# The moving operand of a PE-bound kernel read in 16-byte pieces, by turns from its two halves

## The chip, the cores and the metric

The kernel runs on one core of a Trainium2 chip. Its time is the device time of one execution in microseconds (us); several executions are timed and their median counts. One further execution was recorded by the hardware profiler; the profile and the trace are of that one.

A core has a matrix engine (TensorE, called PE in the profile, with its weight loads as PEld), a vector engine (VectorE, DVE), a scalar engine (ScalarE, ACT), a general engine (GpSimd, POOL) and a queue that issues DMAs (SyncE, SP). They run side by side and wait for each other by semaphores. Operands lie in SBUF, 128 partitions with a row of bytes each; PE writes its results to PSUM, in banks of 512 float32 numbers (2 KB) per partition.

## What is computed

A trunk of two pre-norm residual layers over 512 tokens of 1024 features, in float32, each followed by a squared-ReLU MLP, with RMSNorm at the end. Cut to what matters:

```python
for i in range(2):
    h = rmsnorm(x, norm_mix_g[i])
    h = chunked_spatial_gating(h, ...) if i == 0 else retention(h, ...)
    x = x + h
    h = rmsnorm(x, norm_ffn_g[i])
    a = jax.nn.relu(h @ mlp_w1[i])          # 1024 -> 4096
    x = x + (a * a) @ mlp_w2[i]             # 4096 -> 1024
return rmsnorm(x, final_norm_g)
```

The gating layer has matmuls of 1024 to 4096 and 2048 to 1024 features; the retention has projections of 1024 to 6144 and 2048 to 1024, and inside each of its four heads products of tokens with tokens (scores) and of scores with values.

## The kernel before, in words

Every large product is a sum of three matmuls. Each operand is split into a high part, rounded to PE's float32r format, and a low part, which is the rest; high times high, high times low and low times high are added up in the same PSUM bank. The helper `mm3` (line 213) issues these three: L215, L216 and L217. Its arguments are the PSUM tile `ps`, the stationary operand's two parts `ah` and `al` (128 columns), and the moving operand's two parts `bh` and `bl` (up to 512 columns). A matmul contracts over the 128 partitions, so a product over 1024 features is eight calls of `mm3` into one bank.

Two arrangements use it. With features as the output's partitions (`mm_f`, L303, by `feat`, and `mm_o`, L307, by `out_piece`), a 128x128 piece of weights is stationary and the 512 tokens of the activations move: names `hH`, `hL` (normed input), `aH`, `aL` (MLP activations), `yH`, `yL` (mixer outputs). With tokens as the partitions (`tokens`, L339), 128 tokens are stationary and 512 columns of the weights move: `wH` and `wL`. In the retention's `scores` (L729) and `av` (L749) the moving operand has 512, 384, 256 or 128 columns, since the causal mask leaves less for later chunks. The outputs are named `v`, `u`, `o` (gating layer), `up`, `dn`, `dt` (MLP), `qk`, `vv`, `g`, `sc`, `av`, `ro` (retention). 1912 calls of `mm3` have a moving operand of 512 columns: 5736 matmuls. A few others do not go through it, among them the first 96 matmuls of the gating layer (L562), the norm's sums and spreads (L271, L272, L290, L291), the gate's products `sg` (L474, 128 columns each) and the transposes.

Weights stream in through two 1 MB buffers `raw` (L157), loaded from the SP queue. ACT rounds a piece to `wH` (L179), DVE subtracts to get `wL` (L183); `refill` does so some pieces ahead of PE. PSUM has six banks for accumulation and two for the rest, and results are taken out by DVE and ACT while PE works on other banks. The order is written out by hand: each `step` issues its matmuls, then the preparation of later weights and the pending evacuations.

A tile `fill` of 320 numbers (L130) is never used. It stands ahead of `xT`, `hH` and `hL` in memory and pushes them to multiples of 2 KB. In the built program the moving operand of each 512-column matmul starts at a multiple of 2048 bytes within its partition, so that the two halves of its 2 KB are the two kilobytes of an aligned pair.

Of the kernel before, what the change touches and what calls it, by code (L numbers as in the profile page):

```python
# [78 lines left out]
def trunk(ctx, tc, x, norm_mix_g, norm_ffn_g, a_w_in, a_b_in, a_v_norm_g, a_w_s, a_b_s, a_w_out,  # L79
# [132 lines left out]

    def mm3(ps, ah, al, bh, bl, start, stop):

        nc.tensor.matmul(ps, lhsT=ah, rhs=bh, start=start, stop=False)  # L215
        nc.tensor.matmul(ps, lhsT=ah, rhs=bl, start=False, stop=False)  # L216
        nc.tensor.matmul(ps, lhsT=al, rhs=bh, start=False, stop=stop)  # L217
# [85 lines left out]
    def mm_f(p, ps, bH, bL, ks, last):  # L303
        for k in ks:
            mm3(ps, p.hi[:, k, :], p.lo[:, k, :], bH[k], bL[k], k == 0, k == last)

    def mm_o(p, t, ps, bH, bL):  # L307
        ts = slice(t * P, (t + 1) * P)
        for k in range(4):
            mm3(ps, p.hi[:, k, ts], p.lo[:, k, ts], bH[:, k, :], bL[:, k, :], k == 0, k == 3)  # L310
# [28 lines left out]
    def tokens(plist, bufs, evac, name, behind=None, last=None):  # L339

        accs = {}
        behind = behind or {}

        def one(i):
            def run(p):
                if i == 0:
                    for n in range(NT):
                        accs[n] = acc(f"{name}_{n}")
                aH, aL = bufs()
                for n in range(NT):  # L350
                    s = slice(n * P, (n + 1) * P)
                    for k in range(2):
                        kk = 2 * i + k
                        mm3(accs[n], aH[kk][:, s], aL[kk][:, s], p.hi[:, k, :], p.lo[:, k, :], kk == 0, kk == 7)
                advance()
                refill()
                if i in behind:
                    behind[i]()
                if i == 3:
                    for n in range(NT):  # L360
                        launch(evac(n, accs[n]))
            return run

        for i, p in enumerate(plist[:2] if last else plist):
            step(one(i), p)
        if last:
            step(lambda *ps: last(bufs, accs, evac, *ps), *plist[2:])
# [593 lines left out]
    for k in range(2):  # L961
        p = order[0]
# [56 lines left out]
```

## Time and profile before

| | |
|---|---|
| median of 3 runs | 1406.9 us (1406.83 to 1407.25) |
| the profiled execution's own time | 1407.72 us |
| its span, first to last instruction | 1406.0 us |
| mean granted clock of PE | 0.998 |
| HBM traffic over the span | 95 GB/s |

The profile's page gives the busy time of each engine, the span in 40 slices with a digit for the busy tenths, the chain of work that ended last, and the costliest groups of instructions. In a group's row stand the source line, engine, operation, output and inputs, shapes and count, then the total busy time in us, the mean duration of one in ns, and the idle time of the engine just ahead of them. A matmul's duration is the time that it is in flight; the next starts before it ends. What a matmul costs in a stream is therefore read from the timeline, as the distance from its start to the next one's. A row of the table by stretches has the stretch and its length, then busy time and count of PE, PEld, DVE, ACT and POOL, the granted clock, the DMA engines' share and GB/s.

### The profile page before, as it was taken

Reading aid. Unit: us, or ns where it says so; the run is one execution under the profiler, and the core shown is the slowest. Engines: PE = TensorE matmul, PEld = TensorE weight load, DVE = VectorE, ACT = ScalarE, POOL = GpSimd, SP = SyncE. Lnnn points to the kernel's source line nnn. Section 1 sums busy time; section 2 is a strip of 40 time slices with the busy share of each in tenths; the row PEclk is TensorE's granted clock in tenths of the full one; section 3 lists DMA queues with packets and bytes.
Section 4 is the critical chain, followed back from the end, with each engine's and each line's share of the span. In section 5 each row is a group of like instructions: output and inputs, shape, how many; then the busy total and the mean of one; then the engine's idle time right before and its main releaser. Section 6 shows DMA issues by size and latency. Waiting matters only on the chain.

```text
span 1406.0 us, 15372 instructions
## 1 busy us (share of the span) xinstructions
PE 1390.5 (99%) x6290; PEld 1155.4 (82%) x6290; DVE 793.0 (56%) x1102; ACT 507.2 (36%) x721; POOL 127.7 (9%) x98
## 2 busy tenths in 40 slices
PE   8999999999999999999999999999999999999997
PEld 7888888888888888888888888888888888888885
DVE  6757765775444445476647574564685443434335
ACT  4656633334413223123334323333334422313222
POOL 3010111220000000011111100110130000000002
PEclk9999999999999999999999999999999999999999
DMA  6332222232223322423222131132122332232221
GB/s 225 109 116 90 72 90 88 81 120 90 90 90 104 106 90 90 148 89 108 90 78 72 60 120 60 62 118 90 61 90 91 120 104 90 93 117 91 90 90 60
DMA packets 106101, 135.23 MB, mean 96 GB/s; under 512 B 2400, under 2 KB 79792, under 8 KB 105776
## 3 DMA queue, kind: packets, MB, share of 16 engines
q1 hardware_dynamic: 106000, 134.26, 29.4%
q8 instruction: 49, 0.80, 0.2%
q14 instruction: 20, 0.16, 0.0%
q10 hardware_dynamic: 32, 0.01, 0.0%
HBM read 132.16 MB, written 2.10 MB: 95 GB/s over the span
## 4 chain that ended last, share of the span: by engine, by line
PE 96%; DVE 3%; POOL 0%; ACT 0%; DMA 0%; issue 0%; SPq 0%; ACTq 0%; DVEq 0%
PE up L217 8%; PE up L216 8%; PE up L215 8%; PE dn L217 4%; PE dn L216 4%; PE dn L215 4%; PE dt L216 4%; PE dt L217 4%; PE dt L215 4%; PE g L215 2%; PE qk L215 2%; PE vv L216 2%; PE g L216 2%; PE vv L215 2%; PE g L217 2%; PE vv L217 2%
## 5 line engine op out<-in xcount | busy, mean ns | idle before, releaser
L183 DVE TENSOR_TENSOR wL<-raw,wH 128x1024 fp32r<-128x1024 f32 x239 | 305.9, 1282 | 112.8 <-PE dt L216 65.5
L179 ACT CAST wH<-raw 128x1024 fp32r<-128x1024 f32 x239 | 249.7, 1045 | 264.7 <-PE dt L217 114.9
L215 PE MATMUL up<-hH,wH 128*128 128x512 f32 x480 | 187.2, 390 | 0.0
L217 PE MATMUL up<-hH,wL 128*128 128x512 f32 x480 | 186.8, 389 | 0.0
L216 PE MATMUL up<-hL,wH 128*128 128x512 f32 x480 | 186.8, 389 | 0.0
L631 DVE TENSOR_TENSOR aH<-r 128x512 fp32r<-128x512 f32 x64 | 45.0, 703 | 159.5 <-ACT r L629 159.4
L216 PEld LDWEIGHTS up<-hL,wH 128*128 128x128 f32 x480 | 90.1, 188 | 18.7
L215 PEld LDWEIGHTS up<-hH,wH 128*128 128x128 f32 x480 | 90.1, 188 | 18.7
L217 PEld LDWEIGHTS up<-hH,wL 128*128 128x128 f32 x480 | 90.1, 188 | 18.7
L215 PE MATMUL dn<-aH,wH 128*128 128x512 f32 x256 | 99.6, 389 | 0.0
L216 PE MATMUL dn<-aL,wH 128*128 128x512 f32 x256 | 99.6, 389 | 0.0
L217 PE MATMUL dn<-aH,wL 128*128 128x512 f32 x256 | 99.6, 389 | 0.0
L215 PE MATMUL dt<-wH,aH 128*128 128x512 f32 x256 | 99.6, 389 | 0.0
L216 PE MATMUL dt<-wL,aH 128*128 128x512 f32 x256 | 99.6, 389 | 0.0
L217 PE MATMUL dt<-wH,aL 128*128 128x512 f32 x256 | 99.6, 389 | 0.0
L629 ACT ACTIVATE r<-up 128x512 f32<-128x512 f32 x60 | 35.9, 598 | 166.7 <-PE up L217 166.7
L239 POOL TENSOR_TENSOR ssq<-ssq,sq 128x512 f32<-128x512 f32 x28 | 43.0, 1537 | 401.6 <-ACT sq L238 401.3
L501 DVE TENSOR_TENSOR xs<-dn,wide 128x512 f32<-128x512 f32 x32 | 22.1, 692 | 74.5 <-PE dn L217 74.5
L215 PEld LDWEIGHTS dt<-wH,aH 128*128 128x128 f32 x256 | 48.0, 188 | 10.1
L216 PEld LDWEIGHTS dn<-aL,wH 128*128 128x128 f32 x256 | 48.0, 188 | 10.0
L215 PEld LDWEIGHTS dn<-aH,wH 128*128 128x128 f32 x256 | 48.0, 188 | 10.0
L216 PEld LDWEIGHTS dt<-wL,aH 128*128 128x128 f32 x256 | 48.0, 188 | 9.9
(271 smaller groups left out, 2709.5 us busy)
## 6 DMA issues: line engine op xcount, KB each, us to landing
raw<-in_mlp_w_dram SPq DMA_DIRECT2D x64, 1024.0 KB, 5.1
raw<-in_b_w_in_dram SPq DMA_DIRECT2D x24, 1024.0 KB, 5.0
raw<-in_a_w_in_dram SPq DMA_DIRECT2D x14, 1024.0 KB, 5.2
raw<-in_a_w_out_dram SPq DMA_DIRECT2D x8, 1024.0 KB, 4.9
raw<-in_b_w_out_dram SPq DMA_DIRECT2D x8, 1024.0 KB, 4.9
raw<-in_a_w_in_dram SPq DMA_DIRECT2D x8, 256.0 KB, 6.7
out_dram<-out SPq DMA_DIRECT2D x8, 256.0 KB, 2.1
xr<-in_x_dram SPq DMA_DIRECT2D x3, 512.0 KB, 6.6
```

Of the source, the lines that this page charges most:

```text
L179: nc.scalar.copy(out=p.hi, in_=p.raw.tile[p.view])
L183: nc.vector.tensor_sub(out=p.lo, in0=p.raw.tile[p.view], in1=f32(p.hi))
L215: nc.tensor.matmul(ps, lhsT=ah, rhs=bh, start=start, stop=False)
L216: nc.tensor.matmul(ps, lhsT=ah, rhs=bl, start=False, stop=False)
L217: nc.tensor.matmul(ps, lhsT=al, rhs=bh, start=False, stop=stop)
L239: nc.gpsimd.tensor_tensor(out=state["ssq"], in0=state["ssq"], in1=sq, op=ALU.add)
L501: nc.vector.tensor_mul(t, ps, r2bc)
L629: nc.scalar.activation(r, ps, AF.Relu)
L631: nc.vector.tensor_mul(h, r, r)
```

## The change

Where the moving operand has 512 columns, `mm3` views the output and both moving operands through another access pattern:

```diff
     def mm3(ps, ah, al, bh, bl, start, stop):
 
+
+        if bh.shape[1] == 512:
+            ps, bh, bl = (v.rearrange("p (h l f) -> p l h f", h=2, f=4) for v in (ps, bh, bl))
         nc.tensor.matmul(ps, lhsT=ah, rhs=bh, start=start, stop=False)
         nc.tensor.matmul(ps, lhsT=ah, rhs=bl, start=False, stop=False)
         nc.tensor.matmul(ps, lhsT=al, rhs=bh, start=False, stop=stop)
```

The 512 columns are taken as 2 halves of 64 groups of 4. PE now reads columns 0 to 3, then 256 to 259, then 4 to 7, then 260 to 263, and so on: 16 bytes from each half by turns. The output is written through the same pattern, so that each column's result lies where it lay before. The bytes, the tiles, their places and the engines' other instructions are the same. The matmuls of 384, 256 and 128 columns and those outside of `mm3` keep their pattern.

No instruction changes its place. These are rows of PE's order of work in the MLP of layer 0, of before; `up_0` is the accumulator, `hH` and `hL` the moving parts, `wH` and `wL` the stationary weights:

```order
L215 MATMUL up_0_2632<-hH_101,wH_2546 128x512
L216 MATMUL up_0_2632<-hL_109,wH_2546 128x512
L217 MATMUL up_0_2632<-hH_101,wL_2547 128x512
L215 MATMUL up_0_2632<-hH_102,wH_2546 128x512
L216 MATMUL up_0_2632<-hL_110,wH_2546 128x512
```

And the same place of the changed kernel, whose line numbers are three higher:

```order
L218 MATMUL up_0_2632<-hH_101,wH_2546 128x64x2x4
L219 MATMUL up_0_2632<-hL_109,wH_2546 128x64x2x4
L220 MATMUL up_0_2632<-hH_101,wL_2547 128x64x2x4
L218 MATMUL up_0_2632<-hH_102,wH_2546 128x64x2x4
L219 MATMUL up_0_2632<-hL_110,wH_2546 128x64x2x4
```

The rows, their operands and their order are the same; only the shape of the access pattern differs.

## The prediction

> **What bounds the kernel now.** I read the page's busy table and its rows of slices first, then the chain that ended last, then the matrix engine's waits, and then the timeline of the matrix engine (PE) at single instructions.
>
> ```profile
> span 1406.0 us, 15372 instructions
> PE 1390.5 (99%) x6290; PEld 1155.4 (82%) x6290; DVE 793.0 (56%) x1102; ACT 507.2 (36%) x721; POOL 127.7 (9%) x98
> PE   8999999999999999999999999999999999999997
> PEclk9999999999999999999999999999999999999999
> PE 96%; DVE 3%; POOL 0%; ACT 0%; DMA 0%; issue 0%; SPq 0%; ACTq 0%; DVEq 0%
> ```
>
> PE is busy in every slice, its clock is granted in full, and it makes up 96% of the chain that set the end. A busy share alone would not prove that the matmuls stream without holes, because matmuls overlap, so the waits and the timeline have to say it. The waits of PE by who released them, with total, times and longest:
>
> ```profile
> PE xt L397 <- DMA xr<-in_x_dram: 1.8, 1, 1.8
> PE warm L958 <- POOL ident masks.py:199: 1.4, 1, 1.4
> PE bc_h L290 <- DVE dg_h L286: 0.9, 3, 0.3
> PE st_mix L272 <- POOL st_mix L263: 0.9, 1, 0.9
> ```
>
> That is 5.0 us in 1406. Now the timeline of PE in layer 0's MLP (start, duration):
>
> ```profile
> 329.98 0.39 PE L217 MATMUL up<-hH,wL 128*128 128x512 f32 x1
> ...
> 344.94 0.39 PE L217 MATMUL up<-hH,wL 128*128 128x512 f32 x1
> ```
>
> Between these two rows lie 66 intervals, all of 0.22 or 0.23 us: 14.96 / 66 = 0.2267 us from one 512-column matmul to the next. The 0.39 us printed as a duration is how long one is in flight, not what it costs. So what bounds the kernel is the rate at which 512 columns go through PE, and the change touches exactly that.
>
> **How much of the time the touched matmuls are.** mm3 is called 1912 times with 512 columns, three matmuls each: 5736 of the 6290. At 0.2267 us they take 5736 x 0.2267 = 1300 us of the span. Every nanosecond added to or taken from each is 5.74 us of the kernel. That lever is why even a tiny effect here would be seen: about 0.2% of the time, 2.8 us, is the least that a measurement of this kernel tells from no change, and that is 0.49 ns per matmul.
>
> **What one column costs, and what is left over.** The same lines run matmuls of other widths in the retention's scores, so the profile has durations of the same form at several sizes:
>
> ```profile
> L217 PE MATMUL sc<-qkH,qkL 128*128 128x512 f32 x8 | 3.1, 389 | 0.0
> L217 PE MATMUL sc<-qkH,qkL 128*128 128x384 f32 x8 | 2.7, 340 | 0.0
> L217 PE MATMUL sc<-qkH,qkL 128*128 128x256 f32 x8 | 2.3, 283 | 0.0
> ```
>
> From 256 to 512 columns the time in flight grows by 106 ns, 0.414 ns a column. 512 columns at that rate are 212.0 ns; the measured interval is 226.7. So 14.7 ns of each matmul are not explained by its columns at this slope (an estimate: the two halves of the slope, 57 and 49 ns for 128 columns, differ by 8 ns). Is that a fixed price of an instruction, or one that grows with what is streamed? Narrow matmuls tell:
>
> ```profile
> 717.36 0.33 PE L215 MATMUL av<-pH,vvH 128*128 128x384 f32 x1
> 717.53 0.34 PE L216 MATMUL av<-pL,vvH 128*128 128x384 f32 x1
> ...
> 718.25 0.22 PE L215 MATMUL av<-pH,vvH 128*128 128x128 f32 x1
> 718.31 0.28 PE L216 MATMUL av<-pL,vvH 128*128 128x128 f32 x1
> ```
>
> The first 128-column matmul is followed after 0.06 us; its columns at 0.414 are 53 ns, so some 7 ns are left (to the timeline's 10 ns). The 384-column one is followed after 0.17 us, 159 ns of columns and some 11 left. The remainder gets smaller with fewer columns, so at least part of it comes while columns are streamed. Taken as lost column times, 14.7 / 0.414 = 35 per matmul, one in about 15 columns, some 60 bytes of a partition's row. I can't see in this trace whether that is the read of the moving operand, the write of the result, or neither.
>
> **The change, part by part.** (1) It removes and adds no instruction and no DMA, and moves none: on every engine the built program has the same rows in the same order, and the touched matmuls differ in the shape of two access patterns alone (128x512 becomes 128x64x2x4). (2) The order in which PE takes the columns changes: 4 columns (16 bytes) from the first kilobyte, 4 from the second, and so on: 128 pieces per matmul where there was one run of 2048 bytes. (3) The PSUM side is written in the same order, so each result lands where it did before, and accumulation and evacuation are untouched. (4) The stationary operand is untouched; its load is beside the matmul:
>
> ```profile
> L216 PEld LDWEIGHTS up<-hL,wH 128*128 128x128 f32 x480 | 90.1, 188 | 18.7
> ```
>
> 188 ns in flight in an interval of 227; a matmul made as short as its columns, 212 ns, would still cover it. (5) A longer pattern to decode costs nothing that shows: the 0.06 us step above says that PE can start a new instruction well within a 227 ns interval.
>
> So the price is 5736 times whatever a jump of 1 KB every 16 bytes does to the stream. No matmul in the trace has such a pattern; all read and write one run. Bounds from the nearest rows: below, the whole remainder goes, 5736 x 14.7 = -84 us. Above, a column takes as long as where PE is fed by weight loads, the slowest steady rate of 128-column operands here (this is a piece of the chain):
>
> ```profile
> 220.27 0.89 PE sg L474 x8
> ```
>
> 0.89 / 8 = 0.111 us for 128 columns, 0.87 ns a column, 445 ns for 512: +218 ns each, +1252 us. I take a price of zero. The reason: what PE reads and writes per piece is still whole and consecutive, four columns in a run, the same bytes in the same number of 16-byte pieces, and the nearest row, the 512-column matmul itself, already streams them at within 14.7 ns of its column rate. With zero, the profiled execution stays at its span of 1406.0 us and its own time of 1407.72; the median of the runs shown is 1406.9, 0.8 us below that execution, and the forecast is made for it: 1406.9 us.
>
> [...]
>
> **The rivals.**
>
> *The remainder goes (faster).* If the 14.7 ns come from reading neighbouring pieces one behind the other, taking turns between two places a kilobyte apart may hide it. For it: the remainder grows with the columns. Against: if it is a limit on the data read per time, the order does not matter. Price: -14.7 x 5736 = -84 us, 1323 us. Nothing else takes over as bound: DVE is the next busiest, and in its fullest stretch it has room.
>
> ```profile
> 1000.00:1100.00 100.00, 99.66 (x454) 82.06 (x453) 74.75 (x112) 40.88 (x60) 13.24 (x9) 1.00 0.28 90
> ```
>
> DVE's 74.75 us (the third busy time of the row) would have to fit into 93.5, and the DMA engines stand at a 0.28 share. [...]
>
> *A jump costs a column's time on the read side (slower).* Today's remainder is one lost column in about 15. If it is lost each time the read leaves a stretch of some 64 bytes, then 16-byte pieces lose one every 4 columns: 128 x 0.414 = 53.0 ns in place of 14.7, +38.3 ns, +220 us: 1627 us. It decides from the point where a jump costs over 14.7 / 128 = 0.11 ns. For it: the size of the remainder fits. Against: a read of 16 bytes gives PE work for four columns, 1.66 ns, in which the next address can be fetched.
>
> *The result's write can't follow (slower still).* Each touched matmul adds its result to a PSUM bank in the new order. If each new piece costs a column on top of today's interval, it is +53.0 x 5736 = +304 us, 1711 us; at the rate of the weight-fed rows above, 2659 us. For it: no matmul in the trace writes in pieces, so nothing shows that the write side has room. [...]
>
> That the change does nothing at all is excluded: the patterns stand in the built program.
>
> **How the numbers follow.** No effect: 0.44, at 1406.9, its own range 1404.1 to 1409.7 (0.2% either way). The remainder goes, in whole or in part: 0.22, from 1323 up; one run is the simplest order that a reader of memory can be built for, so that a gain over it seems less likely than a loss. A jump on the read side, in whole or in part: 0.20, up to 1627. The write side, or a read that is worse than one column a jump: 0.14, above that. Leaving out the faster case would alone leave out more than 2 in 10; so the range runs from 1323 to 1627 and leaves out the 0.14 at the top. Faster 0.22, same 0.44, slower 0.20 + 0.14 = 0.34.
>
> **What would show it.** Right: intervals of 0.2267 us in the up stage at the same place of the timeline, the widths of the scores unchanged, and the same span. [...] One look at two neighbouring starts decides. The forecast is wrong if that interval moves by over half a nanosecond.

## The result, and the profile after

The changed kernel takes 1537.74 us (median of 4 runs, 1537.49 to 1538.03) against 1407.08 us of the kernel before in the same comparison: a ratio of 1.0926, with a 95% interval of 1.0907 to 1.0945. It is slower by 130.7 us, where the forecast was no change. The time lies inside of the stated range; the direction was that of the two slower rivals, which had a chance of 0.34 together, 0.20 of it for the read side.

The page of the changed kernel, the lines that answer to those of before:

```profile
span 1535.4 us, 15429 instructions
PE 1521.4 (99%) x6290; PEld 1163.0 (76%) x6290; DVE 792.5 (52%) x1102; ACT 524.0 (34%) x721; POOL 127.3 (8%) x98
PE   9999999999999999999999999999999999999997
PEclk9999999999999999999999999999999999999999
PE 98%; POOL 1%; DVE 0%; DMA 0%; ACT 0%; issue 0%; SPq 0%; ACTq 0%; POOLq 0%
```

PE has as many matmuls as before (6290), its clock is granted in full (0.998), DVE and POOL are busy for as long as they were (792.5 and 127.3 us, 793.0 and 127.7 before), and PE still sets the end, with 98% of the chain. One other engine has changed, though off the chain: ACT is busy for 16.8 us more. Its costliest group rounds the weights and was not touched. Before, then after:

```profile
L179 ACT CAST wH<-raw 128x1024 fp32r<-128x1024 f32 x239 | 249.7, 1045 | 264.7 <-PE dt L217 114.9
L179 ACT CAST wH<-raw 128x1024 fp32r<-128x1024 f32 x239 | 262.3, 1098 | 301.6 <-PE dt L220 128.6
```

One such cast takes 1098 ns where it took 1045. The experiments below say with which half of the change. The waits of PE are no longer than before, 3.7 us in these rows against 5.0:

```profile
PE warm L961 <- POOL ident masks.py:199: 1.4, 1, 1.4
PE xt L400 <- DMA xr<-in_x_dram: 1.2, 1, 1.2
PE st_mix L275 <- POOL st_mix L266: 0.8, 1, 0.8
PE st_mix L274 <- ACT st_mix L265: 0.3, 1, 0.3
```

So the matmuls themselves must have become dearer. The timeline of PE in the same up stage, first and last of 62 starts:

```profile
359.69 0.41 PE L219 MATMUL up<-hL,wH 128*128 128x512 f32 x1
...
374.94 0.42 PE L220 MATMUL up<-hH,wL 128*128 128x512 f32 x1
```

15.25 / 61 = 0.2500 us from one to the next, 23.3 ns more than the 226.7 before. Times 5736 that is 134 us; the span grew by 129.4. (Of the 4 us between, 0.6 are the shorter wait for `xr`. About 2.5 more, by the distances from start to start, are three pauses around the retention's `bc_h`, each of some 0.8 us, which the kernel before had and the changed one lacks.) And only the touched matmuls changed. The scores' groups by shape:

```profile
L220 PE MATMUL sc<-qkH,qkL 128*128 128x512 f32 x8 | 3.3, 416 | 0.0
...
L220 PE MATMUL sc<-qkH,qkL 128*128 128x384 f32 x8 | 2.7, 338 | 0.0
```

512 columns are in flight for 416 ns where it was 389; the 384 columns, which keep their pattern, took 340 and take 338.

### The profile page after: what moved, and what is told of

Read it like the earlier page. It is cut to its first block, busy times and chain, and to the rows that moved or that the text cites. A ratio compares the mean times of both kernels' runs of the same rounds, so it can differ in the third digit from the quotient of the medians.

```text
span 1535.4 us, 15429 instructions
## 1 busy us (share of the span) xinstructions
PE 1521.4 (99%) x6290; PEld 1163.0 (76%) x6290; DVE 792.5 (52%) x1102; ACT 524.0 (34%) x721; POOL 127.3 (8%) x98
## 4 chain that ended last, share of the span: by engine, by line
PE 98%; POOL 1%; DVE 0%; DMA 0%; ACT 0%; issue 0%; SPq 0%; ACTq 0%; POOLq 0%
PE up L219 8%; PE up L218 8%; PE up L220 8%; PE dt L220 4%; PE dn L219 4%; PE dt L219 4%; PE dt L218 4%; PE dn L220 4%; PE dn L218 4%; PE g L218 2%; PE qk L218 2%; PE ro L218 2%; PE g L219 2%; PE ro L220 2%; PE ro L219 2%; PE vv L218 2%
## 5 line engine op out<-in xcount | busy, mean ns | idle before, releaser
L183 DVE TENSOR_TENSOR wL<-raw,wH 128x1024 fp32r<-128x1024 f32 x239 | 305.6, 1279 | 138.4 <-PE dt L219 75.9
L179 ACT CAST wH<-raw 128x1024 fp32r<-128x1024 f32 x239 | 262.3, 1098 | 301.6 <-PE dt L220 128.6
L218 PE MATMUL up<-hH,wH 128*128 128x512 f32 x480 | 199.8, 416 | 0.0
L219 PE MATMUL up<-hL,wH 128*128 128x512 f32 x480 | 199.5, 416 | 0.0
L220 PE MATMUL up<-hH,wL 128*128 128x512 f32 x480 | 199.4, 416 | 0.0
L218 PE MATMUL dn<-aH,wH 128*128 128x512 f32 x256 | 106.4, 416 | 0.0
L219 PE MATMUL dn<-aL,wH 128*128 128x512 f32 x256 | 106.4, 416 | 0.0
L220 PE MATMUL dn<-aH,wL 128*128 128x512 f32 x256 | 106.4, 416 | 0.0
L218 PE MATMUL dt<-wH,aH 128*128 128x512 f32 x256 | 106.4, 416 | 0.0
L220 PEld LDWEIGHTS dn<-aH,wL 128*128 128x128 f32 x256 | 48.4, 189 | 15.6
L220 PEld LDWEIGHTS dt<-wH,aL 128*128 128x128 f32 x256 | 48.4, 189 | 15.6
```

The lines of the kernel that those rows point to most:

```text
L179: nc.scalar.copy(out=p.hi, in_=p.raw.tile[p.view])
L183: nc.vector.tensor_sub(out=p.lo, in0=p.raw.tile[p.view], in1=f32(p.hi))
```

## The experiments

The question was which side pays, the read of the moving operand (theory R) or the write to PSUM (rival W), and after that, what about the order of reading has a price.

**Read alone and write alone.** Each kernel has half of the change:

```diff
+        if bh.shape[1] == 512:
+            bh, bl = (v.rearrange("p (h l f) -> p l h f", h=2, f=4) for v in (bh, bl))
```

```diff
+        if bh.shape[1] == 512:
+            ps = ps.rearrange("p (h l f) -> p l h f", h=2, f=4)
```

> Only the moving operand is read in 16-byte pieces by turns; the result is written as one run, so that the output's columns are permuted (that part of the result is given up). The changed kernel has 250.0 ns from one touched matmul to the next, 23.3 ns over the kernel before. Theory R, the read side pays for the jumps: 250 ns again and 1537 to 1538 us. Rival W, the write to PSUM pays: 226.7 ns and 1407 us. Both sides by halves: about 238 ns and 1472 us.

> The other half of the change alone: the moving operand is read as one run, the result is written to PSUM in 16-byte pieces by turns, so that the output's columns are permuted. Theory R: 226.7 ns and 1407 us. Rival W: 250 ns and 1537 us. If the two sides overlap inside PE, so that each alone is as slow as both, this and the read-only kernel both give 250 ns.

Reading alone in pieces: 1537.54 us, ratio 1.0927 (1.0908 to 1.0945), the whole price. Writing alone in pieces: 1408.02 us, ratio 1.0004 (0.9994 to 1.0013), nothing. The timeline of the up stage with the read in pieces, 49 intervals:

```profile
359.66 0.42 PE L219 MATMUL up<-hH,wL 128*128 128x512 f32 x1
...
371.91 0.41 PE L217 MATMUL up<-hH,wH 128*128 128x512 f32 x1
```

And with the write in pieces, 67 intervals:

```profile
329.67 0.39 PE L218 MATMUL up<-hL,wH 128*128 128x512 f32 x1
...
344.85 0.39 PE L219 MATMUL up<-hH,wL 128*128 128x512 f32 x1
```

250.0 ns against 226.6. Theory R holds, W falls. ACT's cast goes the same way: it takes 1097 ns with the read in pieces alone, against 1045 before. With the write alone its waits for `dt` are those of before, 114.9 us in place of 128.6. So the order of PE's reads also slows an instruction of another engine. The reverse is not what PE pays for: in the MLPs of the changed kernel, matmuls follow each other after 250.00 ns where ACT and DVE were both idle (mean of 1236 intervals), and after 250.05 where both were busy throughout (435 intervals). On the write side pieces smaller than 16 bytes were not tried alone.

**The size of a piece and the distance between the places.** A whole kernel per pattern was not needed: the eight up stages (two layers by four parts) were given names of their own, upa to uph, and each its own pattern. Reading a stage's row: 64 of its 192 matmuls are on one line, so from the first start to the last lie 189 intervals (stages b, c, d, f, g, h; a and e have the norm's matmuls between). Starts are rounded to 0.1 us, which is 0.5 ns here.

```diff
+PATTERNS = {
+    "upa": (turns(2), turns(2)),
+    "upb": (turns(4), turns(4)),
...
+}
     def mm3(ps, ah, al, bh, bl, start, stop):
+        if bh.shape[1] == 512 and state.get("pat"):
+            read, write = state["pat"]
+            ps, bh, bl = write(ps), read(bh), read(bl)
```

> Reading and writing by turns in the up stages of the MLPs alone, with another piece in each of the eight: 8, 16, 32, 64, 128, 256 and 512 bytes from two halves, and 16 bytes from four quarters; all results in their places. Theory J, each jump has a price of 0.18 ns (23.3 ns by 128): 16 bytes 250.0 ns, 32 bytes 238.3, 64 bytes 232.5, 128 bytes 229.6, 256 bytes 228.1, 8 bytes 273. Rival L, the price is that two reads follow each other in pieces too small for a longer fetch: 250 ns at 16 bytes and 226.7 from 32 or 64 bytes on, with no slope behind. Rival B, the two places 1 KB apart get into each other's way: the four quarters, 512 bytes apart, differ clearly from the two halves.

> Up stages alone again, pieces of 16 bytes from two places, written as one run: the halves 1024 bytes apart as in the change, then (second stage) the write side alone as in the change, then places 1008, 992, 960, 896, 768 and 512 bytes apart. The nearer places overlap, so that some columns are read twice and some not at all; the values are wrong and the amount read is the same. Theory B, places whose distance is a multiple of some power of two share a bank and wait for each other: 250 ns at 1024 and 512 bytes, and 226.7 ns or less at 1008 or 992 bytes. Theory J, any jump costs: 250 ns at all distances.

The run on piece sizes; the columns are name, count, time in flight (least/median/most), first and last start:

```profile
L237 PE MATMUL upa<-hH,wH x48: 492/513/514, 302.9 to 351.2; 128*128 128x512 f32 x48
L237 PE MATMUL upb<-hH,wH x64: 412/416/419, 352.2 to 399.5; 128*128 128x512 f32 x64
L237 PE MATMUL upc<-hH,wH x64: 403/408/410, 443.8 to 489.8; 128*128 128x512 f32 x64
L237 PE MATMUL upd<-hH,wH x64: 402/403/404, 534.1 to 579.4; 128*128 128x512 f32 x64
...
L237 PE MATMUL upf<-hH,wH x64: 389/389/478, 1118.2 to 1161.2; 128*128 128x512 f32 x64
L237 PE MATMUL upg<-hH,wH x64: 389/389/390, 1205.4 to 1248.2; 128*128 128x512 f32 x64
L237 PE MATMUL uph<-hH,wH x64: 427/437/441, 1292.4 to 1343.1; 128*128 128x512 f32 x64
```

16 bytes: 47.3 / 189 = 250 ns. 32 bytes: 243. 64 bytes: 240. 256 bytes: 227.5. 512 bytes: 226.5. 16 bytes from four quarters: 268. 128 bytes (upe, where the norm's matmuls lie between): an estimated 236, since its 399 ns in flight lie between 389 at 256 bytes and 403 at 64. So a fixed price per jump falls (theory J): half as many jumps saved 7 ns of 23, a quarter as many 10, and from 256 bytes on no price shows. With 8 bytes (upa) the matmuls follow each other after 340 ns in the timeline (18 intervals from 305.64 us on), far above J's 273; the results were written in 8-byte pieces too, so the run does not say which side pays there. Rival L, no slope from 32 or 64 bytes on, falls too. Rival B has a first point with the quarters.

The run on distances, pieces of 16 bytes:

```profile
L245 PE MATMUL upb<-hH,wH x64: 389/389/402, 339.4 to 382.3; 128*128 128x512 f32 x64
L245 PE MATMUL upc<-hH,wH x64: 407/408/409, 426.5 to 472.5; 128*128 128x512 f32 x64
...
L245 PE MATMUL upf<-hH,wH x64: 403/404/489, 1102.5 to 1147.9; 128*128 128x512 f32 x64
L245 PE MATMUL upg<-hH,wH x64: 412/412/419, 1192.2 to 1239.5; 128*128 128x512 f32 x64
L245 PE MATMUL uph<-hH,wH x64: 412/412/419, 1283.8 to 1331.0; 128*128 128x512 f32 x64
```

upb is the write alone again: 227. 1008 bytes apart (upc): 243, and of the stages not printed, 992 the same, and 960 the same 408 ns in flight. 896 (upf): 240. 768 and 512 (upg, uph): 250, as at 1024. So the same number of jumps of about the same length costs 13 or 23 ns depending on the distance: theory B is nearer than J, though it asked for 226.7 or less at 1008 or 992 and got 243.

**Which distances, and is it the order at all?**

> As the run on distances, with pieces of 16 bytes at 128, 256, 384, 640, 64 and 32 bytes, and with pieces of 64 and of 128 bytes at a distance of 896 bytes (columns partly read twice, values wrong). So far 1024, 768 and 512 bytes gave 250.1 ns, 896 gave 240.5, and 960, 992 and 1008 gave 243.3. Theory P, the memory has a period of 256 bytes: 256 bytes gives 250; 128, 384 and 640 give 240; 64 and 32 give 243. Rival: the far ones differ by chance of what else is read in those stages, and the same distances modulo 256 bytes don't agree. Pieces of 64 bytes at 896: at most the 240.0 that they took at 1024.

```profile
L241 PE MATMUL upb<-hH,wH x64: 406/414/419, 337.0 to 384.2; 128*128 128x512 f32 x64
L241 PE MATMUL upc<-hH,wH x64: 404/404/406, 428.5 to 473.9; 128*128 128x512 f32 x64
...
L241 PE MATMUL upf<-hH,wH x64: 403/403/487, 1102.8 to 1148.2; 128*128 128x512 f32 x64
...
L241 PE MATMUL uph<-hH,wH x64: 394/394/394, 1282.1 to 1326.2; 128*128 128x512 f32 x64
```

256 bytes apart (upb): 250 ns. 384 (upc): 240. 32 bytes (upf): 240, three less than theory P asked for. Of the stages not shown, 640 bytes gave 240 as well, and 128 bytes the same 404 ns in flight as 384. Pieces of 128 bytes at 896 (uph): 233. With the run before: 256, 512, 768 and 1024 bytes all give 250, and 384, 640 and 896 all 240, as does 128 by its time in flight. Stage a itself was in flight for 412 to 419 ns at 1024 bytes, as the stages of 250, and for 404 at 128, as those of 240, so the stage is not what differs. That fits the period of 256 bytes of theory P, as far as these two remainders go. It is not shown beyond them: 64 bytes (upe) were in flight for 406 ns, between the 403 to 405 of the stages at 240 and the 408 of those at 243, where P asked for 243, and no two distances with the same other remainder were run. With pieces of 64 bytes the distance did not matter: 240 at 896 (upg) as at 1024. The halves of the change, 1024 bytes apart, stand at one of the four distances that gave 250.

> Up stages alone, results written as one run, other orders of reading in each of the eight stages; where a place is read again, part of the operand is left out and the values are wrong. Stages a to c read the same 16, 64 and 256 bytes over and over; d reads the run backwards column by column, e backwards in pieces of 64 bytes, f swaps the two 128 bytes of each 256, g swaps the two 16 bytes of each 32, h reads the run as it is. Theory K, what costs is going back to a place that was just read or lies at the same position within 256 bytes: a and b over 226.7 ns, c 226.7, f 226.7, g about 240. Rival N, only the number of turns away from the next address counts: a highest (128 turns), g as high, b and e (32 turns) 240, c and f less. [...]

```profile
L241 PE MATMUL upb<-hH,wH x64: 404/404/408, 334.4 to 379.8; 128*128 128x512 f32 x64
L241 PE MATMUL upc<-hH,wH x64: 389/389/390, 424.0 to 466.9; 128*128 128x512 f32 x64
L241 PE MATMUL upd<-hH,wH x64: 396/397/398, 511.1 to 555.2; 128*128 128x512 f32 x64
...
L241 PE MATMUL upg<-hH,wH x64: 388/392/397, 1181.8 to 1225.9; 128*128 128x512 f32 x64
```

The same 64 bytes over and over (upb): 240 ns. The same 256 bytes (upc): 227, as a plain run. The run backwards (upd) and with the 16 bytes swapped in each 32 (upg): 233, and with the 128 bytes swapped in each 256 (upf) 233 too, where theory K asked for 226.7. And the same 16 bytes over and over, from the timeline of upa, 38 intervals:

```profile
304.36 0.38 PE L241 MATMUL upa<-hH,wH 128*128 128x512 f32 x1
...
312.56 0.38 PE L243 MATMUL upa<-hH,wL 128*128 128x512 f32 x1
```

8.20 / 38 = 215.8 ns. Theory K expected this one above 226.7; it is the fastest of all. The same 64 bytes again and again are slower than a run (240 ns), the same 16 bytes faster. So 10.9 of the 14.7 ns that the prediction called a remainder come with reading different places, even in a plain run. Rival N falls too: swapped pairs turn away 128 times and cost 7 ns, the halves 23.

**Where the operands start.** Both the changed kernel and the one before with 32 bytes more of unused tile:

```diff
-    keep.tile([P, 320], F32, name="fill")
+    keep.tile([P, 328], F32, name="fill")
```

> The changed kernel with 32 bytes more in the unused tile, so that all operands of the 512-column matmuls start 32 bytes behind a multiple of 2 KB. If the price hangs on the distance between the two places alone, 1537.7 us stays; if it hangs on where the operand starts, the time moves.

> The kernel before with the same 32 bytes more. A run of 2 KB passes all positions within 256 bytes wherever it starts: 1407 us. If the remainder of 14.7 ns came from how the operands are aligned, the time would move by some tens of us.

1537.32 us, ratio to before 1.0935 (1.0888 to 1.0982), and 1407.22 us, 1.0000 (0.9988 to 1.0011). A common shift of all operands by 32 bytes moves neither kernel; the multiples of 2 KB are not what costs.

**Larger pieces in the whole kernel.** The change with `f=64`, pieces of 256 bytes from the same two halves:

> The changed kernel with pieces of 256 bytes in place of 16: the same two halves by turns, 8 pieces per matmul in place of 128, in all 5736 matmuls. In the stage of the run on piece sizes this took 227.2 ns; so 1407 us, up to 1410. If a jump of 1 KB has a price in itself, 8 of them at 0.18 ns add 1.5 ns and 8 us: 1415.

1407.45 us, 1.0004 (0.9995 to 1.0014). With pieces of 256 bytes, jumping between the halves is free. The pattern has as many dimensions as that of the change, so its form is not what costs.

**Is there an order that beats the run?** More places, first in single stages:

> Up stages alone, read and written by turns from more places, all results in their places. Pieces of 16 bytes from 8 places 256 bytes apart, 16 places 128 apart, 32 places 64 apart, 64 places 32 apart (all even pieces, then all odd ones); pieces of 32 bytes from 32 places 64 apart and from 16 places 128 apart; pieces of 64 bytes from 16 places 128 apart and from 8 places 256 apart. Theory P, the position within 256 bytes decides: steps of 256 are worst (over 250 ns), steps of 128, 64 and 32 less. If there is an order that beats the plain run, it shows here under 226.7 ns; the least that the same-place run gave is 215.8.

> Up stages alone, read and written in the same order, all results in their places. The one order so far that beats the plain run takes 32 bytes from each of 16 places 128 bytes apart (220.5 ns). Here its neighbours: 32 bytes from 4 places (512 apart) and from 8 (256 apart), 64 bytes from 4 places, 128 bytes from 4 places, the order of 220.5 ns with its places taken from the last to the first, the same with its outer steps from the last to the first, 16 bytes from 32 places from the last to the first, and in the eighth stage the order of 220.5 ns again. Theory P, the position within 256 bytes: the steps of 256 and 512 are slower than the run (240 to 270 ns), the last one repeats 220.5, and the reversed ones show whether the direction counts.

```profile
L237 PE MATMUL upc<-hH,wH x64: 379/385/390, 433.9 to 476.1; 128*128 128x512 f32 x64
L237 PE MATMUL upd<-hH,wH x64: 393/395/396, 520.3 to 564.0; 128*128 128x512 f32 x64
...
L237 PE MATMUL upf<-hH,wH x64: 380/381/466, 1102.2 to 1143.8; 128*128 128x512 f32 x64
```

16 bytes from 32 places 64 bytes apart (upc): 223. From 64 places 32 apart (upd): 231. 32 bytes from 16 places 128 apart (upf): 220. 16 bytes from 8 places 256 apart (upa) were the worst of these, 447 ns in flight and some 278 from one to the next. But the run on more orders did not repeat the best; its eighth stage is the order of 220 again, in another place of the program:

```profile
L245 PE MATMUL uph<-hH,wH x64: 389/391/400, 1276.6 to 1320.2; 128*128 128x512 f32 x64
```

43.6 / 189 = 231 ns. No other of its orders was under 226.7 either: those of the stages b, c, d, f and g took 231 to 258, and a and e were in flight for 393 and 394 ns, where a run takes 389. The two orders in the whole kernel (`h=16, f=8` and `h=32, f=4` in the change's line):

> The changed kernel with 32 bytes from each of 16 places 128 bytes apart, in all 5736 matmuls and on both sides. In one stage this order took 220.5 ns (alternately 219 and 221, 220.0 without the stage's last), against 226.7 of the plain run: 5736 times -6.7 ns is -38 us, 1369 us. If the gain hung on that stage alone (its operands' places), other stages keep 226.7 ns and the time lies between 1369 and 1407 us.

> The changed kernel with 16 bytes from each of 32 places 64 bytes apart, in all 5736 matmuls, read and written in this order. In one up stage this gave 223.5 ns with the single intervals between 218 and 230. If it holds everywhere: 5736 times -3.2 ns, 1389 us. If it falls into a slower rhythm elsewhere, as the order of 32 bytes from 16 places did, 230 ns and 1426 us.

32 bytes from 16 places: 1420.07 us, 1.0080 (1.0063 to 1.0097), slower. Its timeline shows both rhythms, 26 intervals in a down stage and 23 in the retention, just behind matmuls of 128 columns:

```profile
499.81 0.39 PE L220 MATMUL dn<-aH,wL 128*128 128x512 f32 x1
...
505.80 0.39 PE L219 MATMUL dn<-aL,wH 128*128 128x512 f32 x1
...
990.16 0.38 PE L220 MATMUL g<-hH,wL 128*128 128x512 f32 x1
...
995.22 0.38 PE L219 MATMUL av<-pL,vvH 128*128 128x512 f32 x1
```

230.4 and 220.0 ns with the same pattern. The MLPs kept mostly to the slower rhythm (`up` and `dt` are in flight for 391 ns by the median), and the faster one came in the retention (382 in `g`). 16 bytes from 32 places: 1397.89 us, 0.9931 (0.9915 to 0.9948), the one version that beats both kernels, by 0.7%. That is 9.5 us where its one stage promised 18; other stages run slower than that one: from the first to the last start of layer 1's `dt` lie 260.4 us, as many as in the kernel before.

**With the weight load's reads gathered in one place.** That one order has two rhythms made me suspect the weight load, which is in flight beside the matmul, for 188 ns of each interval of 226.7. The stationary operand becomes one column, read 128 times, in stages and in both whole kernels:

```diff
+            ah, al = (bass.AP(v.tensor, v.offset, [list(v.ap)[0], [0, 128]]) for v in (ah, al))
```

> Up stages alone, results written as one run, values wrong: the stationary operand is one column read 128 times (stages a to f), so that a weight load reads one place only; in g and h it reads every fourth column, a new 16-byte piece for each. The moving operand is read a as one run, b as in the change, c in 32-byte pieces from 16 places 128 bytes apart, d in 16-byte pieces from 8 places 256 apart, e the same 64 bytes over and over, f the same 16 bytes over and over, g as one run, h as in the change. So far with plain weights: a 226.7, b 250, c 220 or 230, d 278, e 240, f 215.8. Theory C, the moving operand's reads collide with those of the weight load: a falls to about 215.8, b and e fall clearly, c is one and the same value in all matmuls; g and h rise, since the weight load visits more places. Rival I, the moving read's pieces collide with each other: a to f stay.

> The kernel before with one column read 128 times as the stationary operand of all 5736 matmuls (values wrong). Theory C: up to 10.9 ns less each, -62 us: 1345 us. Rival I: 1407 us.

> The changed kernel with one column read 128 times as the stationary operand (values wrong). Theory C: it comes close to the run above, 1345 to 1407 us. Rival I: 1537 us. A mixture, where both collide: the difference between this and the run above is what the pieces do among themselves.

The whole kernels: the plain run 1425.91 us, 1.0133 (1.0104 to 1.0163), slower; the change 1529.02 us, 1.0866 (1.0834 to 1.0897), a little faster than with plain weights. So the pieces cost 103 us here, 18 ns each, against 131 with plain weights. The stages:

```profile
L251 PE MATMUL upb<-hH,wH x64: 407/408/423, 336.6 to 383.6; 128*128 128x512 f32 x64
L251 PE MATMUL upc<-hH,wH x64: 398/403/403, 427.9 to 473.2; 128*128 128x512 f32 x64
...
L251 PE MATMUL upg<-hH,wH x64: 394/398/401, 1194.8 to 1239.2; 128*128 128x512 f32 x64
L251 PEld LDWEIGHTS upg<-hH,wH x64: 308/310/311, 1194.6 to 1239.0; 128*128 128x128 f32 x64
```

The change's pieces (upb) 249 ns, 32 bytes from 16 places (upc) 240 in place of 220 or 230, the plain run with every fourth column of weights (upg) 235. Of the stages whose rows are not printed, the same 16 bytes over and over (upf) took 216, as before, and the plain run with one column (upa) an estimated 231: its 33.5 us from first to last start, less the 1.0 us that the same stage's pause adds in the run on orders, over 141 intervals. Theory C falls in its main point: the plain run does not get faster, and most of the price of the pieces stays when the weight load visits one place. But rival I, that the weights don't matter, falls as well: one column moves the interval by -1 to +20 ns, while the load stays at 188 or 189 ns in flight. The 235 of upg says less: there the load itself takes 310 ns, longer than the interval, so it may be what holds the matmul up. What the two reads share stays open.

## Why the prediction was wrong

*What bounds the kernel:* right. PE's interval between 512-column matmuls sets the time before and after, and 5736 times its change gives the result within 3%.

*The remainder of 14.7 ns, tied to the columns:* right in kind. 10.9 ns of it go when one place is read again and again, so it belongs to reading. The reading that 384 columns leave only 11 rests on one rounded step; three steps of that timeline, 717.36 to 717.88, give 0.52 / 3 = 0.173 us and some 14 left, about as much as 512 columns. Only the 128-column row shows less.

*Parts 1, 3, 4 and 5 (no instruction moved, results in place, weight load covered, decoding free):* the counts (6290 matmuls), PE's waits (3.7 us) and the runs with pieces on the write side alone and with pieces of 256 bytes (both 1.0004) agree with them. That the weight load lies fully beside the matmul is not the whole story: what it reads moves the matmul's interval, by up to 20 ns with one column.

*Part 2's price of zero:* this step failed. The reason given was that what PE reads per piece "is still whole and consecutive, four columns in a run, the same bytes in the same number of 16-byte pieces". The runs show that whole 16-byte pieces are not enough, since the order in which they are read counts: by turns from two places 1024 bytes apart, pieces of 256 bytes cost 0 ns, of 64 bytes 13 and of 16 bytes 23, and for the 16 bytes the read side alone pays. Why such an order takes longer stays open. In place of a row for a jumping read, which the trace lacked, I took the plain run's interval as a sign of room; the run on orders shows that this read was itself 10.9 ns above the fastest one, so its interval was no such sign.

*The rivals:* the read-side rival had the right place and sign, and too high a price: one lost column per jump, +38.3 ns, against 23.3 measured. Its tie to stretches of 64 bytes was wrong, since pieces of 64 bytes still lose 13 ns. The write-side rival is refuted, by the ratio of 1.0004 for the write alone. The faster rival was wrong for this change, and its thought is not empty: another order of turns gains 0.7%.

## What to carry to other kernels

Where PE streams float32r without waits, as here, the moving operand can stay one run (226.7 ns for 512 columns) or be read in pieces of 256 bytes per partition (1.0004 of the time); 16-byte pieces by turns from two places 256, 512, 768 or 1024 bytes apart took 250 ns, 10% more. The write to PSUM could be permuted in 16-byte pieces for nothing (1.0004). The one order that beat the run gained 0.7%. Before trusting a gain of an access order seen in one stage, run it in the whole kernel: here the same order ran at 220 and at 230 ns.

## What the runs showed of the hardware that was not expected

- The order in which PE reads its moving operand decides between 215.8 ns (one 16-byte place), 226.7 (a plain run), 233 (backwards), 240 to 250 (16 bytes by turns from two places) and 268 (from four quarters) for the same 512 columns.
- With 16-byte pieces from two places, 256, 512, 768 and 1024 bytes between them cost 23 ns (250 in place of 226.7), and 384, 640 and 896 cost 13 (240); 128 has the same 404 ns in flight as 384. Why is not shown.
- The order of PE's reads slows ACT: its cast of 1024 columns takes 1098 ns beside the changed kernel's matmuls and 1045 beside plain ones, while DVE's subtraction stays at 1279 and 1282.
- One order can run in two rhythms, 220.0 and 230.4 ns, in different stretches of one execution, with the clock granted in full (0.997).
- The pattern of the stationary operand changes the matmul's interval: 226.7 ns with plain weights, an estimated 231 in an up stage with one column read 128 times (1.3% on the whole kernel), though the load is in flight for 188 or 189 ns, against 188. Reading every fourth column stretches the load to 310 ns and the interval to 235.
